# A state-space scan whose decay factors are built by a broadcast minimum and biased exponentials, with two weight buffers and other store queues

## The chip, the cores and the metric

The kernel runs on one core of one Trainium2 chip. The metric is device time in microseconds (us) of one execution, as a median of runs. The engines that matter are PE (matrix products, with the weight loads PEld), DVE (elementwise work, with access to PSUM), ACT (activation functions), POOL (elementwise work on SBUF) and SP, whose queue issues the transfers.

## What is computed

Two layers of a trunk over 512 latent and 256 context tokens, width 1024. Layer 0 mixes tokens by a bidirectional state-space scan, layer 1 by neighbourhood attention, and each ends with a squared-ReLU MLP. The change lies in the scan of layer 0. It goes through a sequence in chunks of 128 tokens, for 32 heads in 4 groups and two directions:

```python
def step(state, inp):
    xc, dtc, bc, cc = inp
    cum = jnp.cumsum(dtc * a, axis=1)
    seg = cum[:, :, None] - cum[:, None, :]
    decay = jnp.exp(jnp.where(mask, seg, -jnp.inf))
    cb = jnp.einsum('bign,bjgn->bijg', cc, bc)
    scores = cb[..., None] * decay * dtc[:, None]
    y = jnp.einsum('bijge,bjgep->bigep', scores, xc)
    y = y + jnp.einsum('bign,bgepn->bigep', cc, state) * jnp.exp(cum)[..., None]
    w_end = jnp.exp(cum[:, -1:] - cum) * dtc
    state = state * jnp.exp(cum[:, -1])[..., None, None] + jnp.einsum('bjgn,bjge,bjgep->bgepn', bc, w_end, xc)
    return state, y
```

## The kernel before

All products are in float32, split into a high and a low part, three products for one. A weight unit is a block of 128x1024 numbers: SP loads it into a buffer `raw` (line 104, three buffers that the whole kernel shares), ACT rounds it to `wh` (line 112), DVE takes the rest `wl` (line 113), each with two buffers. PE then runs 48 products for the unit (768 tokens) in `unit` (line 539). 241 such pairs are made over the kernel.

The scan of layer 0 runs beside the products of its own input projection. The outer loop (line 711) goes over the 4 head groups; each has 8 convolution units (`conv_unit`) and, from the third group on, 4 gate units (`z_unit`); 8 more `z_unit`s follow. The scan of a group is a Python generator (`scan`, line 563) that is advanced by `step(1)` at three places inside each weight unit (line 544), so that its work stands between the unit's products. One scan has 29 steps: 6 to make the masks `G` and the transposed tiles, 5 for the backward states, and 18 for its 6 chunks, three each: two half chunks (4 heads, both directions) and one that finishes the chunk. The order in which instructions stand on each engine's queue is set by the framework's scheduler from the program order and its own estimates; each engine then runs its queue in that order and waits at the head of it.

For each of the 48 half chunks `decays` (line 613) makes a tile `E` of 128 x (2 directions x 4 heads x 128) numbers: SP fetches the cumulated sums of 8 heads as rows that are copied to all partitions (line 619, two transfers of 256 KB), DVE subtracts a per-partition number `colb` and takes the minimum with a per-partition `lnd`, in 8 instructions of 128x128 (line 623), ACT takes one exponential over 128x1024 (line 625), DVE multiplies one direction by the mask `G` (line 626), POOL the other (line 627), and POOL adds the two (line 628). PE uses the sum in 4 products of each half chunk (`intra`, line 649). `E` has three buffers and `decays` is called for one half chunk ahead. The third step of a chunk reads `dxs` into `y` (line 654), multiplies the products with the states by `eb` (DVE, line 663), adds `intra` (DVE, line 665) and the two terms (POOL, line 667), and stores `y` to `ypre` (line 668, on SP's queue). `conv_unit` stores its scaled output `zt` to `dxs` (line 560, on SP's queue). `gate` reads `ypre` back later.

On ACT the exponential and the SiLU (lines 556 and 691) use different function tables, so that an ACT_TABLE_LOAD stands at each change between them.

## Time and profile before

| | |
|---|---|
| median of 3 runs | 2216.99 us (2216.97 to 2219.71) |
| profiled execution: time, span | 2219.93 us, 2218.1 us |
| PE busy in the span | 2085.1 us (94%) |
| DVE, ACT, POOL busy | 1336.6, 929.7, 555.0 us |
| scan of layer 0 beside the projection | about 90 to 710 us of the span |
| first MLP, attention, second MLP | about 860 to 1433, 1490 to 1755, 1828 to 2218 us |

PE is busy nearly all the time, so what counts is where it is not, or where its granted clock is below 1. The busy share of the other engines is a mean over stages; in the chunks of the four scans it is far higher than over the span. The profiled execution's time is 2.9 us above the median.

### The profile page before, as it was taken

How to read it: one execution, taken by the hardware profiler on the slowest of the kernel's cores; microseconds unless marked ns; L12 is line 12 of the kernel's file. 1: busy time of each engine (PE TensorE's matmuls, PEld its weight loads, DVE VectorE, ACT ScalarE, POOL GpSimd, SP SyncE). 2: the span in 40 equal slices, each digit the busy share in tenths (PEclk: the TensorE clock that was granted, in tenths of full speed). 3: DMA queues.
4: the chain of work that ended last, by engine and by line, in shares of the span. 5: the costliest groups of instructions: out<-in, count | busy, mean ns of one | idle time of the engine just before them, and what ended most of it. 6: DMA issues, size and time to landing. Idle time of an engine off the chain costs nothing.

```text
span 2218.1 us, 32653 instructions
## 1 busy us (share of the span) xinstructions
PE 2085.1 (94%) x12848; PEld 1742.2 (79%) x12848; DVE 1336.6 (60%) x2311; ACT 929.7 (42%) x1405; POOL 555.0 (25%) x438
## 2 busy tenths in 40 slices
PE   6999898998989988999999999979999989999996
PEld 3787776877877866888888888858898768889895
DVE  5658978689585677413324334398777765344356
ACT  4454544534434644323213223456555644333244
POOL 0024646245453454000000000643222260000003
PEclk8999999999999999999999999989999989999998
DMA  7445756457565722333333221231211114222233
GB/s 262 137 143 177 220 154 202 149 154 200 182 177 163 261 76 78 114 107 114 112 114 115 76 67 58 80 110 48 65 46 50 51 57 153 95 87 95 96 106 114
DMA packets 136877, 269.73 MB, mean 122 GB/s; under 512 B 13074, under 2 KB 70804, under 8 KB 136724
## 3 DMA queue, kind: packets, MB, share of 16 engines
q1 hardware_dynamic: 136724, 267.65, 38.0%
q8 instruction: 101, 1.65, 0.3%
q14 instruction: 52, 0.43, 0.1%
HBM read 244.27 MB, written 23.33 MB: 121 GB/s over the span
## 4 chain that ended last, share of the span: by engine, by line
PE 75%; DVE 13%; POOL 4%; ACT 3%; issue 3%; DMA 2%; SPq 0%; DVEq 0%; ACTq 0%; POOLq 0%
PE acc L837 20%; PE acc L889 20%; PE acc L137 18%; PE a L983 4%; DVE E L623 4%; PE a L994 2%; PE s L162 2%; DMA E<-crow 2%; PE yp L1069 1%; PE pt L1054 1%; PE s L594 1%; DVE wl L113 1%; PE s L253 1%; POOL sxy L299 1%; POOL E L628 1%
## 5 line engine op out<-in xcount | busy, mean ns | idle before, releaser
L112 ACT ACTIVATE wh<-raw 128x1024 fp32r<-128x1024 f32 (+1 forms) x241 | 254.1, 1055 | 675.9 <-PE acc L889 310.0
L113 DVE TENSOR_TENSOR wl<-raw,wh 128x1024 fp32r<-128x1024 f32 (+1 forms) x241 | 315.8, 1311 | 237.0 <-ACT wh L112 233.4
L137 PE MATMUL acc<-hh,wh 128*128 128x512 f32 (+1 forms) x976 | 288.4, 371 | 0.3 <-DVE xT L555 0.3
L137 PE MATMUL acc<-hl,wh 128*128 128x512 f32 (+1 forms) x976 | 264.4, 346 | 0.0
L137 PE MATMUL acc<-hh,wl 128*128 128x512 f32 (+1 forms) x976 | 263.0, 345 | 0.0
L889 PE MATMUL acc<-ah,wh 128*128 128x512 f32 (+1 forms) x832 | 247.7, 347 | 4.1 <-DVE ya L895 4.0
L837 PE MATMUL acc<-hh,wh 128*128 128x258 f32 (+2 forms) x1024 | 242.9, 317 | 8.6 <-ACT hh L367 8.5
L889 PE MATMUL acc<-ah,wl 128*128 128x512 f32 (+1 forms) x832 | 244.8, 344 | 0.8 <-DVE wl L113 0.8
L889 PE MATMUL acc<-al,wh 128*128 128x512 f32 (+1 forms) x832 | 245.1, 344 | 0.0
L837 PE MATMUL acc<-hl,wh 128*128 128x258 f32 (+2 forms) x1024 | 241.4, 314 | 2.9 <-DVE hl L368 2.8
L837 PE MATMUL acc<-hh,wl 128*128 128x258 f32 (+2 forms) x1024 | 240.8, 313 | 0.0
L137 PEld LDWEIGHTS acc<-hh,wh 128*128 128x128 f32 (+1 forms) x976 | 155.8, 190 | 55.0 <-issue 36.4
L623 DVE TENSOR_SCALAR E<-E,colb,lnd 128x128 f32<-128x128 f32 x384 | 171.7, 506 | 33.9 <-DMA E<-crow 33.9
L837 PEld LDWEIGHTS acc<-hh,wh 128*128 128x128 f32 x1024 | 160.9, 192 | 32.4 <-issue 11.5
L299 POOL TENSOR_TENSOR syy<-syy,last 128x512 f32<-128x512 f32 (+2 forms) x24 | 36.3, 1515 | 578.9 <-ACT last L289 578.8
L837 PEld LDWEIGHTS acc<-hl,wh 128*128 128x128 f32 x1024 | 161.2, 191 | 16.7 <-DVE hl L368 4.5
L137 PEld LDWEIGHTS acc<-hh,wl 128*128 128x128 f32 (+1 forms) x976 | 154.2, 190 | 25.1 <-issue 1.2
L137 PEld LDWEIGHTS acc<-hl,wh 128*128 128x128 f32 (+1 forms) x976 | 154.4, 191 | 23.7 <-issue 0.8
L837 PEld LDWEIGHTS acc<-hh,wl 128*128 128x128 f32 x1024 | 162.0, 191 | 11.6 <-issue 0.7
L889 PEld LDWEIGHTS acc<-ah,wh 128*128 128x128 f32 x832 | 139.4, 189 | 32.7 <-issue 13.1
L895 DVE TENSOR_TENSOR ya<-ya,acc 128x768 f32<-128x768 f32 (+2 forms) x56 | 40.6, 725 | 196.7 <-PE acc L889 196.7
L889 PEld LDWEIGHTS acc<-ah,wl 128*128 128x128 f32 x832 | 139.6, 189 | 21.7 <-DVE wl L113 1.0
(318 smaller groups left out, 3806.0 us busy)
## 6 DMA issues: line engine op xcount, KB each, us to landing
raw<-in_w_dram SPq DMA_DIRECT2D x136, 512.0 KB, 3.4
mraw<-in_modw_dram SPq DMA_DIRECT2D x72, 512.0 KB, 3.4
raw<-in_win_dram SPq DMA_DIRECT2D x48, 512.0 KB, 3.8
E<-crow SPq DMA_DIRECT2D x96, 256.0 KB, 5.1
eb<-erow SPq DMA_DIRECT2D x96, 128.0 KB, 3.7
raw<-in_wout_dram SPq DMA_DIRECT2D x24, 512.0 KB, 3.6
raw<-in_modw_dram SPq DMA_DIRECT2D x8, 1024.0 KB, 17.9
raw<-in_wqk_dram SPq DMA_DIRECT2D x16, 512.0 KB, 3.2
```

The lines of the kernel that those rows point to most:

```text
L112: act.activation(wh[:, :n], raw[:, :n], AF.Copy)
L113: dve.tensor_tensor(wl[:, :n], raw[:, :n], wh[:, :n].bitcast(F32), ALU.subtract)
L137: pe.matmul(acc[:m, s0:s1], lhsT=ww[:, i * m:(i + 1) * m], rhs=xx[:, k, s0:s1], start=first and i == 0 and j == 0, stop=last and i == len( ...
L162: mm = pe.matmul(ps[32 * j:32 * j + 32, hf * 256:hf * 256 + 256], lhsT=cact[:, 8 * kg + 2 * j:8 * kg + 2 * j + 32], rhs=raw[:, j * 256:j * ...
L253: pe.matmul(ps[32 * j:32 * j + 32], lhsT=ones[:, :32], rhs=t[i], start=i == 0, stop=i == len(t) - 1)
L299: pool.tensor_tensor(t[:, s0:s1], t[:, s0:s1], d, ALU.add)
L623: dve.tensor_scalar(E[:, d, e], E[:, d, e], colb[:, c, q:q + 1], lnd[:, c, q:q + 1], op0=ALU.subtract, op1=ALU.min)
L837: pe.matmul(acc[:, d0:d0 + s1 - s0], lhsT=ww[wi], rhs=xx[:, k, s0:s1], start=k == 0 and j == 0, stop=k == KB - 1 and j == 2)
L889: pe.matmul(acc[:, s0:s1], lhsT=ww[:, k * P:(k + 1) * P], rhs=xx[:, s0:s1], start=k == 0 and j == 0, stop=k == KB - 1 and j == 2)
L895: dve.tensor_tensor(y, y, acc[:, p0:p1], ALU.add)
L983: pe.matmul(acc[:, :s1 - s0], lhsT=ws[ww][:, k * P:(k + 1) * P], rhs=xx[:, k, s0:s1], start=k == 0 and j == 0, stop=k == KB - 1 and j == 2)
L994: pe.matmul(acc, lhsT=xx[:, k, i * P:(i + 1) * P], rhs=w[ww][:, sl], start=k == 0 and n == 0, stop=k == KB - 1 and n == 2)
```

## The change

The minimum is taken first, against the tile's own cumulated sums: one DVE instruction over 128x1024 with a broadcast operand (`cum`, line 628 of the changed kernel), in place of 8. What was subtracted before comes in as the bias of the exponential (`ncol = lnd - cum`), which differs per head and direction, so ACT runs 8 instructions of 128x128 (line 632). DVE multiplies both directions by `G` in one instruction of 128x1024 (line 633); POOL only adds (line 634). `E` has four buffers. Its rows are fetched by a function of its own (`fetch`, line 616), the first four during the backward states, then three half chunks ahead, and `decays` runs two half chunks ahead, after the products of a half chunk. `raw` has two buffers, not three. `y` is stored from POOL's queue (line 684), `dxs` from ACT's (line 560). The scan's steps stand behind the blocks 1, 3 and 5 of a unit's 8 (counted from 0), not 1, 2 and 4.

```diff
--- before.py
+++ after.py
@@ -101,7 +101,7 @@
 
 
     def wload(src):
-        raw = wpool.tile([P, 1024], F32, tag="raw", name="raw", bufs=3)
+        raw = wpool.tile([P, 1024], F32, tag="raw", name="raw", bufs=2)
         sp.dma_start(raw[:, :src.shape[-1]], src)
         return raw
 
@@ -456,8 +456,8 @@
     ssd = sstack.enter_context(tc.tile_pool(name="ssd", bufs=1))
 
 
-    colb = dk.tile([P, NCH, 64], F32, name="colb")
-    lnd = dk.tile([P, NCH, 64], F32, name="lnd")
+    ncol = dk.tile([P, NCH, 64], F32, name="ncol")
+    cum = dk.tile([P, NCH, 64], F32, name="cum")
     wend = dk.tile([P, NCH, 64], F32, name="wend")
     dec = dk.tile([P, NCH, 64], F32, name="dec")
     dtot = dk.tile([P, NB], F32, name="dtot")
@@ -466,7 +466,7 @@
     w = wsplit(wload(a["wdt"]), 512)
     acc = acc_tile()
     mm3(acc, w, hh, hl, SEG, m=64)
-    draw = ssd.tile([64, T], F32, tag="E", name="draw", bufs=3)
+    draw = ssd.tile([64, T], F32, tag="E", name="draw", bufs=4)
     act.activation(draw, acc[:64, :T], AF.Identity, bias=col("dtb")[:64], scale=1.0)
     ps = sps()
     for c in range(NCH):
@@ -496,6 +496,7 @@
     dta = ssd.tile([P, NCH, 64], F32, tag="sf", name="dta", bufs=2)
     dtv = dt.rearrange("p (c q) -> p c q", q=64)
     dve.scalar_tensor_tensor(dta, dtv, -1.0, arow.unsqueeze(1).broadcast_to([P, NCH, 64]), ALU.mult, ALU.mult)
+    lnd = ssd.tile([P, NCH, 64], F32, tag="sf", name="lnd", bufs=2)
     lndf = lnd.rearrange("p c q -> p (c q)")
     dve.tensor_scalar(lndf, dt, 1.0e-37, None, op0=ALU.max)
     act.activation(lndf, lndf, AF.Ln)
@@ -504,7 +505,6 @@
     pcv = pcum[:, :W].rearrange("p (d c h) -> p d c h", d=2, c=NCH)
     for d in range(2):
         pe.matmul(pcv[:, d], lhsT=tri[:, d * P:(d + 1) * P], rhs=dta[:, :, d * 32:(d + 1) * 32], start=True, stop=True)
-    cum = ssd.tile([P, NCH, 64], F32, tag="sf", name="cum", bufs=2)
     dve.tensor_copy(cum.rearrange("p c (d h) -> p d c h", d=2), pcv)
     ptot = sps()
     pe.matmul(ptot[:, :W], lhsT=ones, rhs=dta.rearrange("p c q -> p (c q)"), start=True, stop=True)
@@ -514,9 +514,9 @@
     dve.tensor_scalar(wend, wend, 0.0, None, op0=ALU.min)
     act.activation(wend, wend, AF.Exp)
     dve.tensor_tensor(wend, wend, dtv, ALU.mult)
-    dve.tensor_tensor(colb, cum, lnd, ALU.subtract)
-    cumT = ssd.tile([64, NCH, P], F32, tag="E", name="cumT", bufs=3)
-    ecT = ssd.tile([64, NCH, P], F32, tag="E", name="ecT", bufs=3)
+    dve.tensor_tensor(ncol, lnd, cum, ALU.subtract)
+    cumT = ssd.tile([64, NCH, P], F32, tag="E", name="cumT", bufs=4)
+    ecT = ssd.tile([64, NCH, P], F32, tag="E", name="ecT", bufs=4)
     for c in range(NCH):
         if c % 2 == 0:
             pt = sps()
@@ -541,7 +541,7 @@
         ws = win.next()
         for k in range(KB):
             mm3(acc, [q[:, k * P:(k + 1) * P] for q in ws], hh, hl, SEG, first=k == 0, last=k == KB - 1, ks=[k])
-            if k in (1, 2, 4)[:n]:
+            if k in (1, 3, 5)[:n]:
                 step(1)
 
     def conv_unit(xb, tag, bufs, n=3):
@@ -557,7 +557,7 @@
         if xb < NB:
             t = zp.tile([P, T], F32, tag="zt", name="zt", bufs=2)
             act.activation(t, o, AF.Copy, scale=dtot[:, xb:xb + 1])
-            sp.dma_start(dxs[xb], t)
+            act.dma_start(dxs[xb], t)
         return o
 
     def scan(g, B, C, X):
@@ -605,31 +605,45 @@
                 dve.tensor_tensor(new, new, ps, ALU.add)
             return new
 
+        def fetch():
+
+            if len(Es) == 12:
+                return
+            ci, hf = divmod(len(Es), 2)
+            E = ssd.tile([P, 2, 4, P], F32, tag="E", name="E", bufs=4)
+            for d in range(2):
+                q0 = d * 32 + g * 8 + hf * 4
+                sp.dma_start(E[:, d], crow[CHUNKS[ci], q0:q0 + 4].partition_broadcast(P))
+            Es.append(E)
+
+        def decays(i):
+
+            if i >= 12:
+                return
+            ci, hf = divmod(i, 2)
+            c, E = CHUNKS[ci], Es[i]
+
+            h0 = g * 8 + hf * 4
+            own = cum[:, c].rearrange("p (d q) -> p d q", d=2)[:, :, h0:h0 + 4].unsqueeze(3)
+            dve.tensor_tensor(E, E, own.broadcast_to([P, 2, 4, P]), ALU.min)
+            for d in range(2):
+                for e in range(4):
+                    q = d * 32 + h0 + e
+                    act.activation(E[:, d, e], E[:, d, e], AF.Exp, bias=ncol[:, c, q:q + 1], scale=1.0)
+            dve.tensor_tensor(E, E, G[c].unsqueeze(2).broadcast_to([P, 2, 4, P]), ALU.mult)
+            pool.tensor_tensor(E[:, 0], E[:, 0], E[:, 1], ALU.add)
+
         back = {5: None}
         order = [5, 4, 3, 2, 1, 0]
+        Es = []
         for i in range(5):
             back[order[i + 1]] = advance(1, order[i], back[order[i]], "sb", 5)
+            if i < 4:
+                fetch()
+            if i >= 3:
+                decays(i - 3)
             yield
-        def decays(ci, hf):
-
-            c = CHUNKS[ci]
-            E = ssd.tile([P, 2, 4, P], F32, tag="E", name="E", bufs=3)
-            for d in range(2):
-                q0 = d * 32 + g * 8 + hf * 4
-                sp.dma_start(E[:, d], crow[c, q0:q0 + 4].partition_broadcast(P))
-            for d in range(2):
-                for e in range(4):
-                    q = d * 32 + g * 8 + hf * 4 + e
-                    dve.tensor_scalar(E[:, d, e], E[:, d, e], colb[:, c, q:q + 1], lnd[:, c, q:q + 1],
-                                      op0=ALU.subtract, op1=ALU.min)
-            act.activation(E, E, AF.Exp)
-            dve.tensor_tensor(E[:, 0], E[:, 0], G[c][:, 0:1].broadcast_to([P, 4, P]), ALU.mult)
-            pool.tensor_tensor(E[:, 1], E[:, 1], G[c][:, 1:2].broadcast_to([P, 4, P]), ALU.mult)
-            pool.tensor_tensor(E[:, 0], E[:, 0], E[:, 1], ALU.add)
-            return E
-
         fwd = None
-        Es = []
         for ci, c in enumerate(CHUNKS):
             cs = slice(c * P, (c + 1) * P)
             eb = ssd.tile([P, 2, 4, P], F32, tag="eb", name="eb", bufs=1)
@@ -640,15 +654,17 @@
             intra = sps()
             for hf in range(2):
                 at = 2 * ci + hf
-                while len(Es) < min(12, at + 1 + 1):
-                    Es.append(decays(*divmod(len(Es), 2)))
+                if hf:
+                    fetch()
                 E = Es[at]
                 for e in range(4):
                     h = hf * 4 + e
                     par, j = h % 2, h // 2
                     pe.matmul(intra[par * 64:(par + 1) * 64, j * P:(j + 1) * P], lhsT=xtok[c][:, h * 64:(h + 1) * 64],
                               rhs=E[:, 0, e], start=True, stop=True)
+                decays(at + 2)
                 yield
+            fetch()
             y = ssd.tile([P, 4, P], F32, tag="y", name="y", bufs=2)
             yf = y.rearrange("p j i -> p (j i)")
             sp.dma_start(y, dxs[g * 4:(g + 1) * 4, :, cs].rearrange("j p i -> p j i"))
@@ -665,7 +681,7 @@
             dve.tensor_tensor(yf, yf, intra, ALU.add)
             for tv in terms:
                 pool.tensor_tensor(yf, yf, tv, ALU.add)
-            sp.dma_start(ypre[g * 4:(g + 1) * 4, :, cs].rearrange("j p i -> p j i"), y)
+            pool.dma_start(ypre[g * 4:(g + 1) * 4, :, cs].rearrange("j p i -> p j i"), y)
             if ci < len(CHUNKS) - 1:
                 fwd = advance(0, c, fwd, "sf", 2)
             yield
```

DVE's queue in the first scan, from the end of one chunk to the next weight unit; L623 and L626 build `E`, L665, L605 and L604 finish a chunk, L113 is `wl` and L554/L555 are the convolution. Before:

```order
L665 TENSOR_TENSOR y<-y,s 128x512
L555 SCALAR_TENSOR_TENSOR xT<-acc,cols,xT 128x255
L623 TENSOR_SCALAR E<-E,colb,lnd 128x128
L663 TENSOR_TENSOR eb<-eb,s 128x512
L623 TENSOR_SCALAR E<-E,colb,lnd 128x128
L605 TENSOR_TENSOR sf<-sf,s 128x512
L623 TENSOR_SCALAR E<-E,colb,lnd 128x128 x13
L604 TENSOR_TENSOR sf<-sf,dec 128x512
L626 TENSOR_TENSOR E<-E,G 128x512 x2
L113 TENSOR_TENSOR wl<-raw,wh 128x1024
```

The same place after, where L628 is the minimum, L633 the product with `G`, and L681 and L679 are the former L665 and L663:

```order
L681 TENSOR_TENSOR y<-y,s 128x512
L605 TENSOR_TENSOR sf<-sf,s 128x512
L633 TENSOR_TENSOR E<-E,G 128x1024
L628 TENSOR_TENSOR E<-E,cum 128x1024
L604 TENSOR_TENSOR sf<-sf,dec 128x512
L113 TENSOR_TENSOR wl<-raw,wh 128x1024
L554 SCALAR_TENSOR_TENSOR xT<-acc,cols,xT 128x511
L681 TENSOR_TENSOR y<-y,s 128x512
L555 SCALAR_TENSOR_TENSOR xT<-acc,cols,xT 128x511
L554 SCALAR_TENSOR_TENSOR xT<-acc,cols,xT 128x255
L633 TENSOR_TENSOR E<-E,G 128x1024
```

The short instructions are gone, and the product of one half chunk stands ahead of the minimum of a later one.

ACT's queue in the first scan, around one weight unit (L112 is `wh`, L552, L556 and L559 the convolution). Before:

```order
L552 ACTIVATE xT<-acc,cols 128x768
L556 ACT_TABLE_LOAD
L556 ACTIVATE xT<-xT 128x768
L559 ACTIVATE zt<-xT,dtot 128x768
L625 ACT_TABLE_LOAD
L625 ACTIVATE E<-E 128x1024 x2
L112 ACTIVATE wh<-raw 128x1024
```

After, with L632 the biased exponentials:

```order
L632 ACT_TABLE_LOAD
L632 ACTIVATE E<-E,ncol 128x128
L112 ACTIVATE wh<-raw 128x1024
L552 ACTIVATE xT<-acc,cols 128x768
L632 ACTIVATE E<-E,ncol 128x128 x7
L556 ACT_TABLE_LOAD
L556 ACTIVATE xT<-xT 128x768
L559 ACTIVATE zt<-xT,dtot 128x768
L632 ACT_TABLE_LOAD
L632 ACTIVATE E<-E,ncol 128x128
L112 ACTIVATE wh<-raw 128x1024
```

The exponentials of one half chunk are now split around `wh`, and the queue holds 71 table loads for the scan's lines in place of 51 (35, 24 and 12 in place of 25, 14 and 12).

SP's queue in the first scan over one chunk (L668 stores `y`, L639 fetches `eb`, L619 fetches `E`, L654 `y`, L196 a modulation weight, L105 a weight unit). Before:

```order
L619 DMA E<-crow 128x512 x2
L668 DMA ypre<-y 128x4x128
L639 DMA eb<-erow 64x4x128 x4
L619 DMA E<-crow 128x512 x2
L196 DMA mraw<-in_modw_dram 128x1024
L654 DMA y<-dxs 128x4x128
L105 DMA raw<-in_win_dram 128x1024
```

After, with L616 for `E`, L653 for `eb` and L670 for `y`:

```order
L616 DMA E<-crow 128x512 x2
L653 DMA eb<-erow 64x4x128 x4
L616 DMA E<-crow 128x512 x2
L196 DMA mraw<-in_modw_dram 128x1024
L670 DMA y<-dxs 128x4x128
L105 DMA raw<-in_win_dram 128x1024
```

The store of `y`, and that of `dxs` further on, no longer stand ahead of the fetches.

## Rows read from the trace of the kernel before

**Rows 1.** Windows over the chunks of four scans: us; busy PE, PEld, DVE, ACT, POOL; clock, DMA

```profile
193.00:266.00 73.00, 65.42 (x428) 50.02 (x424) 69.02 (x134) 36.96 (x38) 44.71 (x31) 0.98 0.73 224
312.00:396.00 84.00, 74.45 (x469) 57.56 (x469) 72.78 (x120) 36.99 (x39) 48.52 (x33) 0.96 0.69 211
466.00:548.00 82.00, 69.18 (x411) 57.05 (x411) 78.44 (x124) 37.36 (x37) 51.78 (x35) 0.92 0.71 198
609.00:697.00 88.00, 78.13 (x457) 64.28 (x458) 74.28 (x119) 37.44 (x38) 46.48 (x30) 0.92 0.60 167
sum 327.00, PE 287.19 PEld 228.90 DVE 294.51 ACT 148.76 POOL 191.49; mean PE 71.80 PEld 57.23 DVE 73.63 ACT 37.19 POOL 47.87
```

**Rows 2.** Waits from 193 to 697 us: who waited for whom, us, times, longest

```profile
ACT E L625 <- DVE E L623: 73.1, 19, 7.2
...
ACT wh L112 <- PE acc L137: 45.8, 13, 6.9
...
PE s L649 <- POOL E L628: 30.6, 16, 4.3
...
DVE E L623 <- DMA E<-crow: 22.8, 6, 6.2
...
PE s L594 <- DVE y L665: 8.7, 4, 4.4
```

**Rows 3.** Waits of SP's queue from 193 to 697 us

```profile
SPq L668 <- POOL y L667: 85.1, 23, 5.5
```

**Rows 4.** The four windows again, for DVE's line 623 alone (first, last, sum)

```profile
193.00:266.00 73.00, 29.42 (x76) 0.98 0.73 224
...
609.00:697.00 88.00, 32.08 (x72) 0.92 0.60 167
sum 327.00, DVE 142.71; mean DVE 35.68
```

**Rows 5.** The four windows for DVE's line 626 alone, their sum

```profile
sum 327.00, DVE 32.34; mean DVE 8.09
```

**Rows 6.** The instructions on tile `raw` from 2009 to 2060 us: ns min/median/max

```profile
L113 DVE TENSOR_TENSOR wl<-raw,wh x9: 1224/1225/1227, 2010.7 to 2056.8; 128x1024 fp32r<-128x1024 f32 x9
...
DMA to landing us min/median/max: 3.1/3.2/4.7
```

**Rows 7.** DVE's groups by line, 466 to 548 us: busy us, mean ns, idle before

```profile
L113 DVE TENSOR_TENSOR wl<-raw,wh 128x1024 fp32r<-128x1024 f32 x5 | 10.1, 2011 | 1.9 <-ACT wh L112 1.9
```

**Rows 8.** The four windows for POOL's line 627 alone, their sum

```profile
sum 327.00, POOL 62.66; mean POOL 15.66
```

**Rows 9.** POOL's timeline from 480 us: start, us

```profile
479.56 1.83 POOL L685 TENSOR_TENSOR ssqy<-ssqy,sq 128x768 f32<-128x768 f32 x1 [2.76 <-ACT sq L684]
```

**Rows 10.** DVE's timeline at the same time

```profile
479.64 1.83 DVE L623 TENSOR_SCALAR E<-E,colb,lnd 128x128 f32<-128x128 f32 x1
```

**Rows 11.** ACT's groups by line and shape, 60 to 700 us

```profile
L625 ACT ACTIVATE E<-E 128x1024 f32<-128x1024 f32 x48 | 50.3, 1058 | 82.4 <-DVE E L623 73.1 <-DVE A L222 5.4 <-POOL E L627 1.9
L625 ACT ACT_TABLE_LOAD x25 | 32.1, 1283 | 33.1 <-DVE E L623 19.3 <-issue 13.3 <-DMA E<-crow 0.3
```

**Rows 12.** ACT's timeline at 1491 us, copies of 128x128

```profile
1491.67 0.30 ACT L1006 ACTIVATE v<-pt 128x128 fp32r<-128x128 f32 x1
1491.82 0.31 ACT L1006 ACTIVATE v<-a 128x128 fp32r<-128x128 f32 x1
```

**Rows 13.** ACT's timeline in the second MLP

```profile
2026.89 1.06 ACT L112 ACTIVATE wh<-raw 128x1024 fp32r<-128x1024 f32 x1 [2.06 <-PE acc L837]
2027.98 0.72 ACT L872 ACTIVATE last<-last,bt 128x512 f32<-128x512 f32 x1
2029.90 0.63 ACT L874 ACTIVATE ah<-last 128x512 fp32r<-128x512 f32 x1 [1.20 <-DVE last L873]
2032.65 1.06 ACT L112 ACTIVATE wh<-raw 128x1024 fp32r<-128x1024 f32 x1 [2.11 <-PE acc L837]
```

**Rows 14.** PE's timeline between the first MLP and the attention

```profile
1440.38 0.64 PE L162 MATMUL acc<-raw,cact 128*32 128x256 f32 x8 [0.65 <-DMA raw<-in_modw_dram]
...
1454.06 1.23 PE L264 MATMUL s<-rows,sel 32*128 32x256 f32 x6 [7.16 <-DVE rows L240]
```

## The prediction

> **What bounds the kernel now.** I read the waits of PE first, then the busy time by stretch, then what the engines in front of PE wait for. PE is busy 94% of the span, so a change can only win where PE waits or where its granted clock is below full. For the scan that is nearly all inside the chunk steps of the four scans. In the four windows over them [rows 1], 327.0 us together, PE is busy 287.2 us: it idles 39.8 us. The granted clock there is 0.98, 0.96, 0.92 and 0.92, so 73 x 0.02 + 84 x 0.04 + 82 x 0.08 + 88 x 0.08 = 18.4 us more go to slow products, behind the idle stretches. The ceiling of any gain in the scan is 39.8 + 18.4 = 58 us, and PE's floor for the four windows 269 us.
>
> Who holds PE there: of the 39.3 us that have a name, 30.6 us are waits of the `intra` products for POOL's sum of `E`, in 16 pieces, and 8.7 us waits for a PSUM bank that DVE frees late [rows 2]. Behind the sum stands a chain: SP's fetch, DVE's 8 short instructions, ACT, DVE and POOL, POOL. ACT waits 73.1 us for line 623, and line 623 itself 22.8 us for the transfer [rows 2]. DVE is busy 294.5 of the 327 us, 95% in the first and 96% in the third window, 87% and 84% in the others [rows 1]. So two things end last by turns: DVE is full, and `E` is fetched late, because SP sits 85.1 us at the store of `y` until POOL has finished it, with the fetches queued behind [rows 3].
>
> **DVE's work on E.** Now: line 623 takes 142.7 us of the four windows, 299 instructions, so 37 half chunks [rows 4], line 626 32.3 us [rows 5]; together 175 us. After: 2 instructions of 128x1024 for each half chunk, 74 in all. None like them is in the trace; the nearest is `wl`, the same width and also with two operands in SBUF. It takes 1.225 us where POOL is quiet [rows 6] and 2.011 us in the third window, beside a busy POOL [rows 7]. That gives 74 x 1.225 = 91 us to 74 x 2.011 = 149 us, and a saving of 84 to 26 us. I take a value between: the 0.79 us that `wl` loses come from POOL, and POOL loses line 627, 62.7 of its 191.5 us [rows 8, 1], a third; 1.225 + 0.79 x 0.67 = 1.75 us, 74 x 1.75 = 130 us, saving 45 us. DVE then has 249 us in the windows, 93% of PE's floor.
>
> **ACT.** 8 exponentials in place of one of 1.058 us [rows 11]. Copies of 128x128 last 0.30 us but start 0.15 us apart [rows 12]; a bias adds about 0.09 us to 128x512 (0.72 against 0.63 us) [rows 13]. So 8 take 8 x 0.15 = 1.2 us if they overlap, 8 x 0.40 = 3.2 us if not: 37 x 0.14 = 5 us to 37 x 2.14 = 79 us more. I take 0.2 us each, 20 us, since these copies too are independent of each other. The 20 more table loads, 1.283 us each [rows 11], add 26 us, some 20 us of it in the windows. ACT goes from 149 us [rows 1] to 189 us (174 to 248 us): under PE's floor at both ends, so nothing for the sum. The Trainium skill (ScalarE: Activation LUTs, What ACT_TABLE_LOAD costs) gives an ACTIVATE with a pointer bias about 280 ns plus 0.833 ns an element, with 93 ns of overlap between neighbours: by it 8 x 0.294 = 2.35 us, and ACT at 217 us, an estimate from that page, still under the floor but nearer to the rival below.
>
> **POOL and the queues.** POOL gives up 63 us in the windows and takes on 24 stores of `y`. No row shows a store from POOL. From below it costs what SP's issue does, next to nothing; from above, POOL's load is 191.5 - 62.7 = 129 us for 20 chunks, 6.4 us each, against PE's 269 / 20 = 13.4 us, so a store may hold POOL up to 7 us before it shows. I take nothing. SP loses the 85.1 us at the store [rows 3], and with `E` fetched three half chunks ahead I expect DVE's 22.8 us for the transfer [rows 2] to go; what is queued next there is `eb`, which still waits for POOL's last addition to `y`. The stores of `dxs` on ACT follow ACT's own copy, so they add no wait there.
>
> **Two weight buffers.** In the second MLP, the tightest stage, `wh` comes every 5.76 us [rows 13]. A `raw` is free when `wl` is done, some 2.3 us after `wh` starts; its new contents land 3.2 us later, 4.7 us at most [rows 6], so 5.5 to 7.0 us after the start, and are wanted 11.5 us after it. Cover: 4.5 us, so nothing; if that is gone, some 200 units pay. Between MLP and attention, where PE takes the modulation weights from `raw` directly, PE already waits 0.65 us for one, but then 7.16 us for DVE [rows 14]: the 8 loads then run in pairs, two buffers a round of some 4 us, and that wait covers most. Price 0 to 4 us; I take 2.
>
> **The sum.** The steps' new places move no work. Of the 58 us I expect two thirds, 39 us: DVE at 249 us is no longer the longest, but it stays at 86% of the 288 us that are left, and in the fourth window PE still idled 9.9 us with DVE at 84% [rows 1], so waits in queue order remain. 39 - 2 = 37 us; the profiled execution, 2219.9 us, goes to 2183 us. The median is 2.9 us below it: **2180 us**.
>
> **Rivals.** (A) ACT's queue order eats half of it. The exponentials of one half chunk stand on both sides of `wh` and of table loads, and ACT waits 45.8 us in 13 pieces for PE at `wh` [rows 2]; DVE's product with `G` then waits for the last exponential, and behind it on DVE stand `wl` and the convolution. For it speaks the new order on ACT, against it that each half chunk is started two ahead, some 13 us. PE idles on as in windows two and four: a third of the ceiling, 19 us, less 2: 2200 us. (B) The same mechanism, slower: it decides from the point where DVE's waits at that product reach (327 - 249) / 20 = 3.9 us a chunk. One wait at `wh` is 3.5 us in the mean and 6.9 us at most [rows 2]; at 5.5 us a chunk the windows take 249 + 110 = 359 us, and the kernel 2217 + 32 = 2249 us. (C) The port. A short instruction of line 623 that met POOL's 1.83 us addition lasted the same 1.83 us and ended with it [rows 9, 10]. If every new DVE instruction met a whole POOL instruction, it would take 1.225 + 1.83 = 3.06 us, 74 of them 226 us; DVE 294.5 - 175 + 226 = 346 us, the windows at DVE's best share of 96% 360 us, the kernel 2250 us. The Trainium skill (SBUF — State Buffer, Who interferes with whom) states that a DVE instruction with two SBUF inputs and a GpSimd instruction that reads SBUF exclude each other for the whole instruction; these two rows agree, while the 0.79 us that `wl` loses in the mean [rows 6, 7] are well short of a whole POOL instruction. (D) The transfers, no change. The bytes are the same. The DMA shares [rows 1] make 53 + 58 + 58 + 53 = 222 us of the windows; in 288 us that would be 77%, and if landings grow so that `E` comes late again, the windows stay as long as they are: 2215 us.
>
> **How the numbers follow.** Forecast 0.64, A 0.15, B 0.06, C 0.05, D 0.10. What a measurement here can tell from no change is about 0.2%, 4.4 us. The forecast and A are faster, D is mostly the same: faster 0.80, same 0.09, slower 0.11. The range reaches from the whole ceiling, 2217 - 58 = 2159 us, over A to 2213 us; B, C and most of D lie outside.
>
> **What would show it.** The chunks of the four scans should take 280 to 300 us, not 327, with PE's wait for POOL's sum under 15 us, no wait of DVE for `E` of note, and a clock above 0.97. The minimum and the product should last 1.3 to 2.0 us each; over 2.5 us it is C. ACT's exponentials should start 0.15 to 0.30 us apart; DVE idle before the product with `G`, over 2 us a chunk, is A or B. SP should have no wait for POOL's `y` except at `eb`. The MLPs and the attention should stand still within 4 us; if they are longer, the third weight buffer was needed. The forecast is wrong if `E` is ready and PE still idles, that is if PSUM or the states hold it.

## The result, and where the time went

The changed kernel takes **2249.07 us** (2247.74 to 2252.12), the kernel before 2216.98 us: the ratio is **1.0144, with a 95% interval of 1.0127 to 1.0162**. It is 32 us slower, where 37 us faster was forecast, and it lies outside the range of 2159 to 2213 us.

Where it went is seen by cutting the span at products that both kernels have: the first product of the first scan, the last product with a state (end of the scans), the first product of the first MLP, of the attention's values, of its scores, of the second MLP. Windows of the kernel before (us; busy PE, PEld, DVE, ACT, POOL; granted clock, DMA share, GB/s):

```profile
137.70:709.10 571.40, 531.29 (x3232) 430.66 (x3232) 443.14 (x742) 255.70 (x292) 272.37 (x186) 0.97 0.59 175
709.10:841.90 132.80, 121.87 (x657) 98.97 (x655) 91.36 (x103) 71.39 (x106) 65.48 (x47) 0.96 0.49 169
841.90:1462.50 620.60, 599.26 (x3578) 491.65 (x3576) 253.24 (x342) 180.31 (x255) 71.94 (x42) 0.98 0.30 96
1462.50:1501.80 39.30, 35.98 (x222) 32.44 (x223) 31.88 (x74) 23.11 (x55) 4.32 (x7) 0.93 0.21 65
1501.80:1813.10 311.30, 295.69 (x1856) 256.48 (x1855) 233.82 (x570) 185.23 (x399) 98.07 (x121) 0.98 0.18 57
1813.10:2218.10 405.00, 383.57 (x2584) 346.96 (x2584) 202.12 (x282) 144.19 (x195) 37.46 (x29) 0.97 0.31 102
```

The same six windows of the changed kernel (span 2247.7 us):

```profile
137.00:723.80 586.80, 534.94 (x3233) 432.82 (x3232) 384.85 (x427) 339.10 (x621) 229.95 (x161) 0.95 0.56 170
723.80:862.60 138.80, 124.14 (x658) 101.74 (x656) 91.45 (x103) 71.58 (x106) 66.32 (x48) 0.94 0.47 161
862.60:1483.90 621.30, 599.48 (x3576) 490.22 (x3574) 254.38 (x346) 181.12 (x257) 72.55 (x43) 0.98 0.29 95
1483.90:1527.30 43.40, 37.21 (x224) 33.53 (x225) 31.61 (x71) 21.40 (x53) 5.73 (x6) 0.87 0.27 83
1527.30:1839.40 312.10, 296.89 (x1855) 257.15 (x1854) 233.70 (x570) 185.13 (x399) 98.06 (x121) 0.98 0.18 57
1839.40:2247.70 408.30, 384.25 (x2584) 346.24 (x2584) 201.64 (x283) 143.77 (x195) 34.59 (x29) 0.97 0.31 102
```

Of the 29.6 us between the spans, the scans lose 15.4, the stretch behind them up to the first MLP (the seam) 6.0, the start of the attention 4.1 and the second MLP 3.3; the rest is under 1 us each. In the scans DVE works 58 us less (443.14 to 384.85), as intended, and POOL 42 us less; PE idles 51.9 us (586.80 - 534.94) in place of 40.1, and its products take 3.65 us longer, at a granted clock of 0.95 in place of 0.97. So the work went and the waits grew.

Which ones, the waits tell (who waited for whom: us, times, longest). In the kernel before, from 137 to 842 us:

```profile
SPq L668 <- POOL y L667: 86.9, 24, 5.5
DVE E L623 <- DMA E<-crow: 28.8, 8, 6.2
PE s L179 <- ACT row L177: 0.5, 1, 0.5
```

The changed kernel, from 137 to 863 us:

```profile
SPq L653 <- POOL y L683: 142.7, 23, 12.0
DVE E L628 <- DMA E<-crow: 67.6, 22, 7.2
PE s L663 <- POOL E L634: 24.1, 7, 7.9
PE s L663 <- DVE eb L679: 12.2, 3, 6.2
PE s L179 <- ACT row L177: 8.7, 2, 5.0
```

SP's wait for POOL's last addition to `y` was 86.9 us at the store; it has moved to the next fetch of `eb` (line 653) and grown to 142.7 us. DVE's wait for `E` was 28.8 us in 8 pieces; it is 67.6 us in 22. PE's wait for POOL's sum fell from 30.6 us in 16 pieces [rows 2] to 24.1 in 7, each longer. Two others joined it: one for `eb`, and one of 8.7 us in two pieces for `row`, a copy that ACT makes for the modulation products.

One place shows the whole. The changed kernel's timeline from 640 us, first the last additions to `y` on POOL, then SP, DVE, ACT and PE (start, us, engine, line; in brackets the idle time before it and what ended it):

```profile
644.89 2.26 POOL L683 TENSOR_TENSOR y<-y,eb 128x512 f32<-128x512 f32 x1
```
```profile
647.18 3.32 SPq L653 DMA_DIRECT2D eb<-erow  x4
650.60 1.03 SPq L616 DMA_DIRECT2D E<-crow  x2
```
```profile
650.56 0.68 DVE L681 TENSOR_TENSOR y<-y,s 128x512 f32<-128x512 f32 x1
658.39 1.23 DVE L628 TENSOR_TENSOR E<-E,cum 128x1024 f32<-128x1024 f32 x1 [7.16 <-DMA E<-crow]
659.54 0.68 DVE L679 TENSOR_TENSOR eb<-eb,s 128x512 f32<-128x512 f32 x1
660.14 1.22 DVE L633 TENSOR_TENSOR E<-E,G 128x1024 f32<-128x1024 f32 x1
```
```profile
651.46 1.57 ACT L632 ACTIVATE E<-E,ncol 128x128 f32<-128x128 f32 x5
659.65 2.45 ACT L632 ACTIVATE E<-E,ncol 128x128 f32<-128x128 f32 x8 [6.62 <-DVE E L628]
```
```profile
640.18 0.66 PE L663 MATMUL s<-E,xtok 128*64 128x128 f32 x8
665.74 1.12 PE L663 MATMUL s<-E,xtok 128*64 128x128 f32 x8 [7.88 <-POOL E L634]
```

The next `E` goes into the buffer of four half chunks earlier, which by count is free when the products at 640.18 are through, at 640.8. Its fetch starts at 650.60, because on SP it stands behind the four `eb` fetches, which wait for POOL until 647.1 and take 3.3 us to issue. It lands at 658.3. DVE has its minimum next in its queue and stands still for 7.16 us. Behind the minimum stands the product at 660.14, of the half chunk *before* that one: its last exponential was done at 653.0. POOL's sum of that product is what PE waits 7.88 us for at 665.74. And the `eb` term behind the minimum is what POOL's next `y` waits for (over the kernel POOL waits 66.7 us for DVE there, 50.9 us before), which holds the next `eb` fetch on SP. The wait feeds itself. This was not a rare place: counted on DVE's timeline, 32 of the 48 minima stand ahead of a product of an earlier half chunk. The Trainium skill (TensorE: Matmul & The Clock Gate, Architectural detail: the array is 16× 32×32, not 1× 128×128) calls ScalarE's and VectorE's queues strict FIFO; the trace agrees, with 7.16 us of idle DVE ahead of a product that could have run.

The late `E` reaches PE through ACT's queue as well. One of the two waits for `row`, DVE, ACT and PE of the changed kernel:

```profile
387.25 1.23 DVE L628 TENSOR_TENSOR E<-E,cum 128x1024 f32<-128x1024 f32 x1 [5.12 <-DMA E<-crow]
```
```profile
388.51 1.86 ACT L632 ACTIVATE E<-E,ncol 128x128 f32<-128x128 f32 x6 [9.10 <-DVE E L628]
392.10 0.36 ACT L177 ACTIVATE row<-s 128x256 f32<-128x256 f32 x1
```
```profile
392.51 0.44 PE L179 MATMUL s<-consts,row 128*128 128x128 f32 x2 [4.97 <-ACT row L177]
```

The copy stood behind six exponentials, a `wh` and a convolution on ACT's queue, and the exponentials behind the minimum.

### The profile page after: what moved, and what is told of

It reads as the page before. It is cut to its first block, busy times and chain, and to the rows that moved or that the text cites. A ratio compares the mean times of both kernels' runs of the same rounds, so it can differ in the third digit from the quotient of the medians.

```text
span 2247.7 us, 32592 instructions
## 1 busy us (share of the span) xinstructions
PE 2094.6 (93%) x12848; PEld 1746.7 (78%) x12848; DVE 1277.0 (57%) x1975; ACT 1021.9 (45%) x1761; POOL 512.5 (23%) x414
## 4 chain that ended last, share of the span: by engine, by line
PE 77%; DVE 8%; DMA 6%; POOL 3%; ACT 3%; issue 2%; SPq 1%; DVEq 0%; ACTq 0%; POOLq 0%
PE acc L137 20%; PE acc L853 20%; PE acc L905 19%; PE a L999 4%; DMA E<-crow 2%; PE a L1010 2%; PE s L162 2%; PE yp L1085 1%; PE s L594 1%; DVE wl L113 1%; PE pt L1070 1%; PE s L663 1%; PE s L253 1%; PE s L677 1%; ACT wh L112 1%
## 5 line engine op out<-in xcount | busy, mean ns | idle before, releaser
L112 ACT ACTIVATE wh<-raw 128x1024 fp32r<-128x1024 f32 (+1 forms) x241 | 254.1, 1055 | 680.8 <-PE acc L905 302.6
L113 DVE TENSOR_TENSOR wl<-raw,wh 128x1024 fp32r<-128x1024 f32 (+1 forms) x241 | 311.6, 1293 | 275.3 <-ACT wh L112 271.7
L137 PEld LDWEIGHTS acc<-hh,wh 128*128 128x128 f32 (+1 forms) x976 | 158.0, 193 | 61.3 <-issue 39.5
L632 ACT ACTIVATE E<-E,ncol 128x128 f32<-128x128 f32 x384 | 122.2, 391 | 102.0 <-DVE E L628 86.6
L905 PEld LDWEIGHTS acc<-al,wh 128*128 128x128 f32 x832 | 139.6, 189 | 20.0
```

What stands on the lines that cost most here:

```text
L112: act.activation(wh[:, :n], raw[:, :n], AF.Copy)
L113: dve.tensor_tensor(wl[:, :n], raw[:, :n], wh[:, :n].bitcast(F32), ALU.subtract)
L137: pe.matmul(acc[:m, s0:s1], lhsT=ww[:, i * m:(i + 1) * m], rhs=xx[:, k, s0:s1], start=first and i == 0 and j == 0, stop=last and i == len( ...
L632: act.activation(E[:, d, e], E[:, d, e], AF.Exp, bias=ncol[:, c, q:q + 1], scale=1.0)
L905: pe.matmul(acc[:, s0:s1], lhsT=ww[:, k * P:(k + 1) * P], rhs=xx[:, s0:s1], start=k == 0 and j == 0, stop=k == KB - 1 and j == 2)
```

## The experiments

The theory from this reading was the loop: late decay, DVE's product and `eb` terms held behind the minimum, late `y`, late `eb` fetch, late decay; and beside it a price of the two weight buffers. The rivals were that the buffers are the whole loss, and that ACT's slower arithmetic is. The scheduler plans the whole program anew for every edit, so an edit that fixes one order can shift others (e12's scan lines have 75 table loads, those of the changed kernel 71); no run separates that. The table gives the measured median, the difference to the kernel before as measured beside it, and from the profile the stretch of the four scans (as above), PE's idle time in it, and DVE's whole wait for `E`, in us. "Queue theory" in the expectations is the loop.

| kernel | median | to before | scans | PE idle | DVE for E |
|---|---|---|---|---|---|
| before | 2216.98 | | 571.4 | 40.1 | 33.9 |
| after | 2249.07 | +32.1 | 586.8 | 51.9 | 70.9 |
| e1_two_raw | 2232.01 | +12.5 | 571.4 | 41.0 | 33.8 |
| e2_stores | 2242.17 | +22.7 | 593.2 | 55.2 | 48.2 |
| e3_arith | 2247.11 | +27.6 | 601.4 | 65.7 | 64.8 |
| e4_no_arith | 2247.77 | +28.3 | 584.9 | 49.8 | 30.0 |
| e5_eb_late | 2216.68 | -3.2 | 553.7 | 32.0 | 26.5 |
| e6_eb_pool | 2217.44 | -2.4 | 560.3 | 33.2 | 36.0 |
| e7_fetch | 2232.63 | +12.8 | 570.7 | 39.7 | 31.0 |
| e8_raw3 | 2233.12 | +13.3 | 583.7 | 52.8 | 70.0 |
| e9_late_raw3 | 2207.14 | -13.0 | 556.1 | 31.5 | 26.8 |
| e10_late_old | 2259.67 | +39.5 | 597.9 | 60.8 | 33.8 |
| e11_late_sp | 2235.51 | +15.3 | 573.7 | 42.4 | 54.9 |
| e12_min_behind | 2210.21 | -10.0 | 547.0 | 26.6 | 9.4 |
| e13_both | 2221.67 | +1.3 | 560.5 | 35.0 | 10.6 |
| e14_behind_raw3 | 2193.33 | -27.0 | 544.3 | 25.9 | 7.7 |
| e15_arith_behind | 2223.10 | +2.8 | 579.7 | 46.8 | 31.7 |
| e16_both_raw3 | 2207.75 | -12.6 | 562.3 | 34.2 | 9.2 |
| e17_best_old | 2254.14 | +33.4 | 604.5 | 65.5 | 22.7 |
| e18_best_sp | 2191.08 | -29.6 | 543.6 | 23.2 | 5.4 |

### Each part alone

**e1_two_raw**, in the kernel before:

```diff
-        raw = wpool.tile([P, 1024], F32, tag="raw", name="raw", bufs=3)
+        raw = wpool.tile([P, 1024], F32, tag="raw", name="raw", bufs=2)
```

> The kernel before with two raw weight buffers instead of three and nothing else. Queue theory (the loss in the scans comes from the decay fetches, which stand on SP's queue behind the eb fetch and reach a VectorE that now waits for them with its whole queue; two raw buffers cost only the seams outside the scans): 2225 to 2230 us, 8 to 13 us above the kernel before, most of it between the last scan and the first MLP and at the start of the attention. Buffer theory (two raw buffers are the whole loss): 2240 to 2250. Arithmetic theory (ScalarE's eight exponentials per half chunk, their table loads and the wide operations are the whole loss): 2215 to 2219.

12.5 us slower (ratio 1.0060, 1.0043 to 1.0077), and the scans not at all: 571.4 us as before. So the buffers are a cost, and not the whole loss. By the six windows the seam takes 136.7 us (+3.9), the attention's start 43.6 (+4.3), the second MLP 408.9 (+3.9). The second place can be read. SP of the kernel before, then of this one, ahead of the attention's first products:

```profile
1446.11 1.18 SPq L105 DMA_DIRECT2D raw<-in_wv_dram  x2
```
```profile
1458.14 0.35 SPq L105 DMA_DIRECT2D raw<-in_wv_dram  x1
1465.68 0.35 SPq L105 DMA_DIRECT2D raw<-in_wv_dram  x1
```

And PE of this one:

```profile
1464.48 0.58 PE L1109 MATMUL pt<-wh,hh 128*128 128x256 f32 x1 [4.57 <-ACT wh L112]
1468.37 0.58 PE L1109 MATMUL pt<-wl,hh 128*128 128x256 f32 x1 [3.10 <-DVE wl L113]
```

The third buffer let the first value weights in 16 us before their use, across the stretch where modulation weights hold buffers. Without it they come 6 us before it, and PE waits.

**e2_stores**, in the kernel before:

```diff
-            sp.dma_start(dxs[xb], t)
+            act.dma_start(dxs[xb], t)
...
-            sp.dma_start(ypre[g * 4:(g + 1) * 4, :, cs].rearrange("j p i -> p j i"), y)
+            pool.dma_start(ypre[g * 4:(g + 1) * 4, :, cs].rearrange("j p i -> p j i"), y)
```

> The kernel before with its y stores issued by GpSimd and its dxs stores by ScalarE and nothing else. Queue theory: SP's wait of 85 us for the last addition to y does not go, it moves from the store to the next eb fetch; the time stays within 8 us of the kernel before, 2209 to 2225. Buffer theory and arithmetic theory: 2215 to 2219. If the time falls below 2205, moving the stores is a gain that other parts of the change took away again.

All three were wrong: 22.7 us slower, all of it in the scans. That the wait moves was right, as SP's waits of this kernel say (136 to 864 us):

```profile
SPq L639 <- POOL y L667: 78.1, 22, 6.1
```

Line 639 is the `eb` fetch. DVE's wait for `E` grows from 33.9 to 48.2 us. This run alone doesn't tell what makes that so dear; e18_best_sp below bears on it.

**e3_arith**, in the kernel before, only these lines of `decays` (and the tiles `ncol` and `cum` for them):

```diff
+            dve.tensor_tensor(E, E, own.broadcast_to([P, 2, 4, P]), ALU.min)
             for d in range(2):
                 for e in range(4):
...
-                    dve.tensor_scalar(E[:, d, e], E[:, d, e], colb[:, c, q:q + 1], lnd[:, c, q:q + 1],
-                                      op0=ALU.subtract, op1=ALU.min)
-            act.activation(E, E, AF.Exp)
-            dve.tensor_tensor(E[:, 0], E[:, 0], G[c][:, 0:1].broadcast_to([P, 4, P]), ALU.mult)
-            pool.tensor_tensor(E[:, 1], E[:, 1], G[c][:, 1:2].broadcast_to([P, 4, P]), ALU.mult)
...
+                    act.activation(E[:, d, e], E[:, d, e], AF.Exp, bias=ncol[:, c, q:q + 1], scale=1.0)
+            dve.tensor_tensor(E, E, G[c].unsqueeze(2).broadcast_to([P, 2, 4, P]), ALU.mult)
```

> The kernel before with the new arithmetic alone (one wide minimum, eight exponentials with bias, one wide product); the fetch stays one half chunk ahead with three E buffers, the stores stay on SP, three raw buffers. Queue theory: VectorE works some 45 us less, its waits for decays stay, so 2200 to 2220. Arithmetic theory: 2235 to 2250. Buffer theory: under 2215.

27.6 us slower, as the arithmetic theory had it and against the two others, and the largest DVE saving of all runs beside it: DVE works 375.36 us in the scans, 68 less than before. Its wait for `E` is 64.8 us. So either ACT's part costs that much, or the wide minimum's place does; e12, e15 and e17 were made to tell these apart.

**e4_no_arith** is the changed kernel with the old arithmetic (the bias added by DVE as the second operation of its eight instructions, half of the product with `G` on POOL again):

```diff
-            dve.tensor_tensor(E, E, own.broadcast_to([P, 2, 4, P]), ALU.min)
...
+                    dve.tensor_scalar(E[:, d, e], E[:, d, e], cum[:, c, q:q + 1], ncol[:, c, q:q + 1],
+                                      op0=ALU.min, op1=ALU.add)
+            act.activation(E, E, AF.Exp)
+            dve.tensor_tensor(E[:, 0], E[:, 0], G[c][:, 0:1].broadcast_to([P, 4, P]), ALU.mult)
+            pool.tensor_tensor(E[:, 1], E[:, 1], G[c][:, 1:2].broadcast_to([P, 4, P]), ALU.mult)
```

> The changed kernel with the old arithmetic put back (VectorE adds the bias in eight 128x128 operations, one 128x1024 exponential, product with G half on VectorE and half on GpSimd); fetch three half chunks ahead, two raw buffers and the moved stores stay. Queue theory: the loss stays, and VectorE's 45 us more come on top in part: 2245 to 2270. Arithmetic theory: 2215 to 2225. Buffer theory: 2240 to 2250.

+28.3 us: without the arithmetic the change loses as much as with it. The arithmetic theory, which said 2215 to 2225, falls as a whole account.

**e7_fetch** is e4_no_arith with both stores back on SP, that is the kernel before with the fetch and `decays` further ahead, four `E` buffers, the new steps and two `raw` buffers:

```diff
-            act.dma_start(dxs[xb], t)
+            sp.dma_start(dxs[xb], t)
...
-            pool.dma_start(ypre[g * 4:(g + 1) * 4, :, cs].rearrange("j p i -> p j i"), y)
+            sp.dma_start(ypre[g * 4:(g + 1) * 4, :, cs].rearrange("j p i -> p j i"), y)
```

> The kernel before with two raw buffers, the fetch three half chunks ahead with four E buffers and the moved scan steps, but the old arithmetic and both stores on SP. To be set beside the kernel before with two raw buffers alone (2232 us, scans 571 us). Queue theory: SP waits at the y store as before and the decay fetch is issued earlier, so VectorE's wait for decays falls from 29 us to under 20, scans 562 to 572, time 2222 to 2233. Rival (the new places of the fetch and of the steps are themselves the loss): scans 580 or more, 2242 to 2250.

The same as e1_two_raw (2232.63 against 2232.01 us; scans 570.7 against 571.4). With the old arithmetic these parts together neither cost nor gain; DVE's wait for `E`, 31.0 us, did not fall under 20 as expected.

### The loop, cut at either end

**e5_eb_late**: SP issues the decay fetch first (`lastE` is its last transfer), `eb` behind it. The changed kernel with

```diff
...
-            for par in range(2):
-                for d in range(2):
-                    sp.dma_start(eb[par * 64:(par + 1) * 64, d], ev[par, d].partition_broadcast(64))
...
                 if hf:
                     fetch()
+                    with tc.issue_after(lastE[0]):
...
+                                sp.dma_start(eb[par * 64:(par + 1) * 64, d], ev[par, d].partition_broadcast(64))
```

> The changed kernel with one order changed: on SP's queue a chunk's four eb fetches, which wait for GpSimd's last addition to y of the chunk before, are issued behind the decay fetch of that chunk and no longer ahead of it. Queue theory, after four runs: the scans lose because the decay fetches stand behind the eb fetches and VectorE's wide minimum, which waits for them, stops the products and eb terms queued behind it; so VectorE's wait for decays falls from 68 us to under 25, the four scans from 587 us to 572 to 578, the time to 2235 to 2241. Rival (VectorE's and ScalarE's own order: the wide minimum and the eight exponentials come late in any case): VectorE's wait falls as well but turns into waits for ScalarE's exponentials, scans 583 to 590, time 2246 to 2252.

32 us come back with one order, more than the theory's 8 to 14; DVE's wait for `E` in the scans is 24.4 us, as expected, and the scans fall further than expected, to 553.7 us.

**e6_eb_pool**: `eb` fetched by POOL, which makes the `y` it waits for.

```diff
-                    sp.dma_start(eb[par * 64:(par + 1) * 64, d], ev[par, d].partition_broadcast(64))
+                    pool.dma_start(eb[par * 64:(par + 1) * 64, d], ev[par, d].partition_broadcast(64))
```

> The changed kernel with the 96 eb fetches issued by GpSimd, whose own last addition they wait for, so that SP's queue never waits for it. Queue theory: VectorE's wait for decays falls to under 25 us; GpSimd pays 96 issues of 0.6 to 0.8 us, 58 to 77 us over the scans, some of it ahead of the sums that TensorE waits for: 2235 to 2250. Rival (order on VectorE and ScalarE): 2250 to 2265, the issues on GpSimd added and nothing won.

The same gain by another way (2217.44 us, below both ranges), though POOL pays 96 issues of 0.617 us, 59 us; DVE's wait was expected lower than 36.0 us.

**e12_min_behind** leaves SP alone and cuts on DVE: `prods` holds the products of the scan.

```diff
-            dve.tensor_tensor(E, E, own.broadcast_to([P, 2, 4, P]), ALU.min)
+            with tc.issue_after(prods[-1]) if prods else nullcontext():
+                dve.tensor_tensor(E, E, own.broadcast_to([P, 2, 4, P]), ALU.min)
...
-            dve.tensor_tensor(E, E, G[c].unsqueeze(2).broadcast_to([P, 2, 4, P]), ALU.mult)
+            prods.append(dve.tensor_tensor(E, E, G[c].unsqueeze(2).broadcast_to([P, 2, 4, P]), ALU.mult).ins)
```

> The changed kernel, its fetches as late as they are, with one order changed on VectorE: each wide minimum is issued behind the product of the half chunk before it, so that a minimum that waits for its transfer no longer holds that product. If what a late decay costs is the product and the eb terms held behind the minimum: 2225 to 2238. If the decays themselves come too late for their own products, whatever stands behind the minimum: 2243 to 2250, VectorE's wait for decays as long as before or longer. If the products now hold the queue in turn while they wait for ScalarE's exponentials: above 2250.

2210.21 us, 39 us below the changed kernel and more than any theory said. Its waits, 137 to 684 us:

```profile
PE s L664 <- POOL E L635: 21.7, 11, 4.6
DVE E L634 <- ACT E L633: 14.7, 13, 3.7
DVE E L629 <- DMA E<-crow: 9.4, 4, 3.7
```
```profile
SPq L654 <- POOL y L684: 86.5, 22, 8.1
```

The edit leaves SP's order of `eb` and `E` as it was, yet its wait for `y` falls from 142.7 to 86.5 us and DVE's for `E` to 9.4: with the product no longer behind the minimum, `y` is early, and so are `eb` and the next `E`. PE's wait for ACT's `row` is gone too (0.8 us in the whole kernel). The price, DVE at the product waiting for ACT, is 14.7 us. ACT works *more* within these scans than in the changed kernel:

```profile
137.20:684.20 547.00, 520.44 (x3234) 422.99 (x3233) 389.23 (x429) 356.23 (x648) 237.73 (x160) 0.98 0.60 181
```

**e13_both** has the edits of e5_eb_late and e12_min_behind.

> The changed kernel with both orders changed: on SP the decay fetch ahead of the eb fetches (alone 2216.7 us), on VectorE each minimum behind the product before it (alone 2210.2). If the two are links of one loop (a late decay holds VectorE's product, that makes GpSimd's y late, that holds eb and with it the next decay on SP), cutting the second link adds little: 2205 to 2212. If they are two losses beside each other: 2178 to 2190.

The gains don't add, which speaks for one loop and against two losses beside each other. But 2221.67 us lies outside both ranges: that the second cut makes it 11 us slower than e12 alone was not expected. In its profile DVE waits 12.7 us for `eb` to land against 5.4 in e12, and SP 62.6 us for PE to free an `E` buffer against 38.3, with `eb` now queued behind that; this fits, but was not tested further.

### The buffers again, and what each part is worth in the right order

**e8_raw3**: the changed kernel with three raw buffers, for which one of the eight `xtok` tiles goes.

```diff
-        raw = wpool.tile([P, 1024], F32, tag="raw", name="raw", bufs=2)
+        raw = wpool.tile([P, 1024], F32, tag="raw", name="raw", bufs=3)
...
-            xtok[c] = ssd.tile([P, 512], F32, tag="xtok", name="xtok", bufs=8)
+            xtok[c] = ssd.tile([P, 512], F32, tag="xtok", name="xtok", bufs=7)
```

> The changed kernel with three raw weight buffers again, the room taken from the token tiles xtok, seven in place of eight. All theories after the run with two raw buffers alone: the 10 to 13 us behind the scans come back, at the seam before the first MLP, at the start of the attention and in the second MLP: 2236 to 2240. If the seventh xtok tile delays the start of a scan, up to 5 us more.

16 us back, a little more than e1 lost. **e9_late_raw3** (with e5's edit), **e14_behind_raw3** (with e12's) and **e16_both_raw3** (with both) gain 10, 17 and 14 us over the same kernels with two buffers, so this price stands apart from the loop. e16 lies outside both its ranges, as e13 did; e9, at 2207.14 us, lies 1 us above the case in which the gains add.

> The changed kernel with the decay fetch ahead of the eb fetches on SP and three raw buffers (seven xtok tiles). If the two causes found so far are separate, the gains add: 2216.7 less 13 to 16, so 2200 to 2206, below the kernel before. If they share a cause: 2210 to 2217.

> The changed kernel with each minimum behind the product before it and three raw buffers (seven xtok tiles). If the buffers' cost is apart from the loop, as two pairs of runs say (13 and 16, and 10 us): 2194 to 2201. Otherwise 2207 to 2211.

> The changed kernel with both orders changed and three raw buffers (seven xtok tiles). One loop: 2192 to 2201. Two losses: 2165 to 2178.

e14_behind_raw3 is faster than both kernels: **2193.33 us, ratio 0.9882 (0.9864 to 0.9900)**.

**e15_arith_behind** puts e12's order into e3_arith:

> The kernel before with the new arithmetic alone (2247.1 us in the order that its scheduling gave it) and each minimum behind the product before it; the fetch one half chunk ahead, three E and three raw buffers, the stores on SP. If the arithmetic loses by VectorE's order alone and is otherwise worth what was predicted: 2195 to 2215. If ScalarE's eight exponentials and table loads lose the time: 2235 to 2250. If the fetch is needed ahead as well: 2215 to 2235.

2223.10 us: 24 of the 27.6 us are gone, so ACT's exponentials were not what e3 lost. But no gain is left. PE waits 45.6 us for POOL's sum there, and SP 96.6 us for PE to free an `E`: the time lies in the third case, where the fetch is needed ahead as well. What e18_best_sp below has more than this kernel (fetch three and `decays` two half chunks ahead, four `E` buffers, the new steps) is worth 32 us, though the same parts gave nothing with the old arithmetic (e7); which of them counts was not tested.

**e17_best_old** takes the new arithmetic out of e14 (e4's lines, the eight instructions held behind the product), **e10_late_old** takes it out of e5:

> The fastest version so far (the changed kernel with each minimum behind the product before it and three raw buffers, 2193.3 us) with the old arithmetic, its eight bias operations behind the product as the minimum was. What the new arithmetic is worth where VectorE's order is right: as predicted, two thirds of VectorE's 45 us, 2215 to 2230; all of it and more, as in the pair with the order changed on SP (43 us), 2230 to 2245; nothing, 2190 to 2200.

> The changed kernel with the decay fetch ahead of the eb fetches on SP, but the old arithmetic. To be set beside the same order with the new arithmetic (2216.7 us). If the new arithmetic relieves VectorE as predicted once the decays are in time, this one is slower, 2222 to 2235, with TensorE waiting for VectorE's y and eb terms. Rival (the arithmetic moves nothing on the path): 2213 to 2220.

2254.14 us against 2193.33, a difference of 61 us; 2259.67 against 2216.68, 43 us. Both are slower than any case expected. But the old arithmetic loses by these orders themselves: e5's order on SP makes it 12 us slower (e10 against e4_no_arith), and the moved stores cost the kernel before 22.7 us (e2). So 61 and 43 us are no price of the arithmetic alone. In e17 PE waits for DVE's `y` (19.2 us), its `eb` (8.8), and the scans' window shows why, DVE 474.80 us where e14 has 390.74:

```profile
134.90:739.40 604.50, 539.02 (x3234) 434.16 (x3233) 474.80 (x758) 268.91 (x303) 283.86 (x209) 0.95 0.54 164
```
```profile
138.60:682.90 544.30, 518.38 (x3235) 420.75 (x3233) 390.74 (x429) 356.28 (x648) 238.39 (x160) 0.99 0.59 182
```

**e18_best_sp** puts both stores of e14 back on SP (the diff of e7_fetch), **e11_late_sp** those of e5:

> The fastest version so far (2193.3 us) with both stores back on SP. If moving the stores is worth what it was with the order changed on SP (19 us): 2207 to 2217. If with VectorE's order right SP's wait at the y store no longer reaches VectorE: 2190 to 2200.

> The changed kernel with the decay fetch ahead of the eb fetches on SP, but both stores back on SP. Queue theory: SP waits at the y store for GpSimd's last addition and the decay fetches stand behind that again: VectorE's wait for decays over 35 us, 2225 to 2240. Rival (where the stores stand does not matter once eb is out of the way): 2213 to 2220.

2191.08 us (ratio 0.9865, 0.9849 to 0.9882): no loss, though SP stands at the store for 89.6 us again. In e11, with DVE's own order, the same move costs 19 us. Waits of e18, SP and DVE, 138 to 682 us:

```profile
SPq L685 <- POOL y L684: 89.6, 23, 7.7
```
```profile
DVE E L629 <- DMA E<-crow: 5.4, 5, 1.8
```

So SP's wait, which the prediction named as the reason that `E` is late, does no harm in this kernel, where the fetch is three half chunks ahead and DVE doesn't put the minimum first.

## Why the prediction was wrong, point by point

- **DVE's work on E: right, the total in part by luck.** 1.75 us an instruction was forecast, 1.53 and 1.49 measured (below). 45 us for 37 half chunks is 58 us for 48, and DVE's scans fell by 58.3 us; but the work on `E` alone fell by 72.2 us in that stretch (lines 623 and 626 before, 212.4 us; 628 and 633 after, 140.2), and other DVE instructions took 14 us more. Rival C (3.06 us each) fell. C's row showed an instruction that reads one tile [rows 10]; those of the change read two, and lasted 1.21 us at least and 2.88 us at most. What the relief is worth depends on the order: nothing in the scheduler's own (after against e4_no_arith), and with the order mended 27 to 30 us from the kernel before to e14 and e18, of the forecast "two thirds", 39 us.
- **ACT: the exponentials too low, with little effect of their own.** Eight take 2.45 us, 0.306 each, not 0.2: they last 0.39 us and start 0.294 us apart. The table loads of the scan's lines are 71 for 51, the 20 more that were forecast. The Trainium skill (ScalarE: Activation LUTs, What ACT_TABLE_LOAD costs) gave 8 x 0.294 = 2.35 us, an estimate close to the 2.45 measured. Rival A had DVE's product wait for them, over 2 us a chunk; it waited 5.3 us in all. What ACT's queue did cost, PE's 8.7 us at `row`, came at the place shown from exponentials that waited for the minimum; with the minimum behind the product it is 0.8 us (e12). Groups of the changed kernel, 60 to 730 us (busy us, mean ns, idle before):

```profile
L632 ACT ACTIVATE E<-E,ncol 128x128 f32<-128x128 f32 x384 | 122.2, 391 | 102.0 <-DVE E L628 86.6 <-issue 5.3 <-PE s L162 4.9
L628 DVE TENSOR_TENSOR E<-E,cum 128x1024 f32<-128x1024 f32 x48 | 73.5, 1533 | 75.9 <-DMA E<-crow 70.9 <-POOL ssqy L701 2.9 <-POOL xw L592 1.0
L633 DVE TENSOR_TENSOR E<-E,G 128x1024 f32<-128x1024 f32 x48 | 71.5, 1493 | 5.3 <-ACT E L632 5.3
L684 POOL DMA_DIRECT2D ypre<-y x24 | 18.8, 785 | 5.9 <-POOL y L683 5.6 <-DMA yg_d<-zt 0.3
```

- **POOL and the queues: the step that failed.** "I expect DVE's 22.8 us for the transfer [rows 2] to go; what is queued next there is `eb`, which still waits for POOL's last addition to `y`." DVE's wait did not go; over the whole scans it grew from 28.8 to 67.6 us. The second half names the wait that came, 142.7 us, and no price was put on it; the decay fetch stands behind that one as it stood behind the store. The step also asked only when `E` lands and not what stands behind its reader: the minimum, ahead of the product of the half chunk before. Undoing that alone brings 39 us (e12), undoing SP's order alone 32 (e5). SP's order shown with the change has the fetch of `E` behind that of `eb`. DVE's order shown there, from the first scan, has a product ahead of the minimum and was taken for the rule; at 658 us, and in 32 of 48 half chunks, it is the other way round. That a store costs POOL next to nothing was right as an issue (0.785 us each; e14 and e18 take the same time).
- **Two weight buffers: 0 to 4 us forecast, 12.5 measured.** The cover was worked out for the steady second MLP and for PE's modulation products. In the MLP it held: in e1, PE is busy from 1900 to 2100 us without a gap. The price lies at the seams, where a third buffer let the next stage's first weights in early; "that wait covers most" looked at the wrong products. Of the rest, the second MLP's 3.9 us lies at its two ends, has no one large wait to show for it and stays unexplained.
- **Rivals.** D had "`E` comes late again" with no change in time, but by full transfer engines. The DMA share in the scans fell from 0.59 to 0.56. A fetch of `E` did land later, 6.1 us after its issue in the median against 5.0, but in e14, the kernel with the order mended, it takes 6.0 us: what costs is the order, not the longer landing. B gave 2249 us, the measured time, by a wait that did not occur. None was a wait that feeds itself.
- **The size.** With the order mended, e12 stands 10 us below the kernel before, 13 of buffers included; e14 and e18, with the buffers back, 27 and 30 us below. That is what was right of the 37. e17, e14 with the old arithmetic, is 33 us slower than the kernel before, so the gain needs the new arithmetic.

## What to carry to other kernels

An operation made wide gains what its duration says only if it also keeps its place: one wide instruction that waits for a whole transfer holds everything behind it in its engine's queue, so put it behind the work whose inputs are ready. When a store or fetch is moved off a queue that waits, look for the next instruction on that queue with the same wait, and price it. A shared buffer that seems idle in the steady loop may be carrying the prefetch across a seam between stages.

## What was not expected of the hardware

POOL took 96 more transfer issues (0.617 us each, 59 us) in e6_eb_pool without a loss that shows beside e5, where SP issues them (2217.44 and 2216.68 us). And PE's idle time was paid twice here: from e14 to e17 PE idles 39.6 us more in the scans (25.9 to 65.5), and the granted clock falls from 0.99 to 0.95, so that the same products take 20.6 us longer (518.38 to 539.02).
